# RG-LRU gates in TensorE's two row halves, with rope, w_mod and norm steps moved in a two-layer hybrid encoder

## The chip, the cores and the metric

One core of a Trainium2 chip runs the whole kernel. The metric is the time of one execution on the device, in microseconds (us); the program has one launch. The engines are TensorE (PE, with its weight loads shown apart as PEld), VectorE (DVE), ScalarE (ACT), GpSimd (POOL) and SyncE (SP, which here only issues DMAs).

## The reference

Two groups of 256 tokens go through two layers with shared weights, all in float32. One layer, cut to what the change touches:

```python
def rglru_branch(x_in, gate_in, conv_w, conv_b, w_a, b_a, w_i, b_i, lam):
    xc = dwconv_centred(x_in, conv_w, conv_b)
    xb = xc.reshape(B, S, RG_BLOCKS, RG_BW)            # 8 heads of 64
    def direction(d, reverse):
        r = sigmoid(einsum('bsnc,ncd->bsnd', xb, w_a[d]).reshape(B, S, RG_WIDTH) + b_a[d])
        i = sigmoid(einsum('bsnc,ncd->bsnd', xb, w_i[d]).reshape(B, S, RG_WIDTH) + b_i[d])
        ...
def encoder_layer(x, c, cos, sin, p):
    mod = (silu(c) @ p['w_mod'] + p['b_mod'])[:, None, :]
    sh1, sc1, gt1, sh2, sc2, gt2 = split(mod, 6, axis=-1)
    h = rmsnorm(x, p['ln1_g']) * (1 + sc1) + sh1
    ...                                  # h @ w_in, attention with rope, RG-LRU, gated DeltaNet
    x = x + gt1 * (mixed @ p['w_out'])
    h2 = rmsnorm(x, p['ln2_g']) * (1 + sc2) + sh2
    up = dwconv_centred(h2 @ p['ffn_w_up'], p['ffn_conv_w'], p['ffn_conv_b'])
    x = x + gt2 * ((silu(u_gate) * u_lin) @ p['ffn_w_down'])
```

## The kernel before

Both groups are laid side by side, so an activation tile is 128 channels by 512 tokens. A weight matrix is cut into **units** of 128 x 128, and the units of a layer stand in the order in which they are used; eight make a **chunk** of 512 KB. A chunk is loaded by SP into a `raw` buffer (four of them), cast by ACT to a high part `wh`, and DVE forms the low part `wl`. A unit then takes three matmuls (`mm3`): high weight on high and on low activations, low weight on high. `gemm` runs eight units into one PSUM bank; the pool `mm` has three banks, and ACT or DVE must have read a bank before a later job takes it. A chunk's load is issued two chunks ahead, and ACT's cast is called for six units ahead of use.

The order on TensorE and on SP is written by the program itself. `JOBS` lists the gemms of a layer: `in6` (first projections), attention (`uq`, `uk`, `uv`), the gated DeltaNet (`gq`, `gk`, `gv`, `z`), RG-LRU (`x` input, `g` gate, `b.i.d` recurrence gates of block i and direction d), `gate`, `br` (branches), `out`, `up`, `down`. Between units a `Driver` polls small generator tasks: attention steps, the DeltaNet chain (`solve`, `combine`: tiles `gdn_*`), and the modulation. Each task yields an estimated delay from `SLACK` or an event, and runs when the driver's own clock `now` has passed it. ACT, DVE and POOL are ordered by the framework's scheduler.

**Modulation.** `mod_gen` computes silu(c) @ w_mod. A w_mod chunk is four matmuls with 32 weight columns each, one in each quarter of TensorE's columns (tile `mod`, eight records in the trace). When a group of four blocks' columns is done, ACT copies the bank (`modev`), and four small matmuls select the rows (`mod<-cs,modev`). Layer 0 runs blocks 0 to 3 at the start; both layers run 4 to 9 (24 chunks) during the branches, one chunk every 8 us and loaded through the same `raw` buffers as the weights; 10 and 11 run in the norm ahead of `up` from `oraw` tiles. Blocks 0 to 3 of layer 1 run during `down` of layer 0 and in the norm behind it. Work in `drv.spare` is run wherever the driver has to wait.

**Gates of RG-LRU** (`rg_scan`): two heads of 64 are put on the diagonal of a 128 x 128 unit, one unit for w_a and one for w_i, three matmuls each, into banks `zr` and `zi`; ACT reads each with one tanh of 128 x 512.

**Rope** (`query`, `place`): DVE rotates the queries into tile `rope`; SP writes them to DRAM (`drope`) and back into `Qt`, at times that the driver's clock sets.

**Norms**: a sum of squares by TensorE, DVE's reciprocal square root (`tsx`), a matmul that spreads it over the partitions (`norm<-cs,tsx`), and `modulated`: DVE multiplies, ACT scales and shifts (`hn`), POOL makes the high part `hh`, DVE the low part `hl`.

Of the kernel before, what the change touches and what calls it, by code (L numbers as in the profile page):

```python
# [18 lines left out]
P = 128  # L19
T = 512  # L20
S = 256
# [21 lines left out]
def jobs():  # L43
# [10 lines left out]
        "gate": 8, "br": 4, "x": 8, "g": 8, "b": 2, "z": 8, "out3": 24, "out": 8, "up3": 24, "up": 8,  # L54
# [5 lines left out]

SLACK = {
    "modev": 0.7, "att_s": 3.2, "att_t": 1.8, "att_e": 1.0, "low_rank": 11.8, "low_rank_out": 152.5, "mla": 0.2,
# [3 lines left out]
    "rg_all": 16.0, "ssq": 6.5, "kq": 8.0, "norm": 2.8, "normed": 17.0, "mod1": 8.0, "mod2": 8.0,  # L66
# [75 lines left out]
class Driver:  # L142
# [12 lines left out]
    def spawn(self, gen):  # L155
        self.tasks.append([self.now, gen])
        self.poll()
# [12 lines left out]
    def poll(self):  # L170
        for task in list(self.tasks):
            if task in self.tasks and self._ready(task[0]):
                self._step(task, self.tasks)

# [61 lines left out]
def _body(es, tc, nc, xT, cT, wall, wmod, pvec, fng, cst, rope, xinit, yT, dbg):  # L236
# [348 lines left out]
    def modulated(l, which, x, r, k, g, h, pool, bufs):  # L585
        modT, modA = mods[l]
        c = GS[g]
        scale, bias = modA[:, which, k, g:g + 1], modT[:, 24 * which + k, g:g + 1]
        t = pool.tile([P, S], F32, name="hn", tag="hn", bufs=bufs)
        mul(t, x[:, c], r)  # L590
        A.activation(t, t, AF.Identity, bias=bias, scale=scale)  # L591
# [3 lines left out]
        split(t, h[k][0][:, c], h[k][1][:, c], pool=True)  # L595
# [45 lines left out]
    def hs(h):  # L641
        return [h[k] for k in range(8)]
# [71 lines left out]
    for l in range(depth):  # L714
# [84 lines left out]
        def query(j):  # L799
            if j == 0:  # L800
                drv.until(ev_cq)
            ps = gemm(cq)
            if j < 4:
                A.activation(Qt[0:64, 2 * j, :], ps[0:64], AF.Copy, scale=96.0 ** -0.5)
                A.activation(Qt[0:64, 2 * j + 1, :], ps[64:128], AF.Copy, scale=96.0 ** -0.5)
                return
            cosq, sinq = rep2(rt_[:, 0, :]), rep2(rt_[:, 1, :])
            if j == 4:
                lr["rope"] = mp.tile([P, 4, T], F32, name="rope", tag="Vt")
            ab = lr["rope"][:, 2 * j - 8:2 * j - 6, :]  # L810
            mul(halves(ab[:, 0, :]), halves(ps), cosq)
            mul(halves(ab[:, 1, :]), halves(ps), sinq)
            if j == 5:
                x, y = lr["rope"][:, 0:2, :], ab
                sub(x[:, 0, :], x[:, 0, :], y[:, 1, :])
                add(x[:, 1, :], x[:, 1, :], y[:, 0, :])

                def place():
                    yield SLACK["rope"]
                    dr = dp.tile([P, 2, T], F32, name="drope", tag="drope")  # L820
                    nc.sync.dma_start(dr, x)
                    yield SLACK["rope_out"]
                    for e in range(2):
                        nc.sync.dma_start(Qt[64 + 16 * e:80 + 16 * e], dr.rearrange("(h p) e t -> e p h t", p=16)[e])
                    ev_q.set(SLACK["rope_in"])
                drv.spawn(place())
# [102 lines left out]
        def rg_scan(i, d):  # L929
# [3 lines left out]
            zr = gemm([(xh, xl)])  # L933
            zi = gemm([(xh, xl)])
# [7 lines left out]
            A.activation(s, zr, AF.Tanh, bias=pr["hb"][:, c:c + 1], scale=0.5)  # L942
            A.activation(u, zi, AF.Tanh, bias=pr["hb"][:, 8 + c:9 + c], scale=0.5)
# [130 lines left out]
        def ahead():  # L1074
            yield from modulation(l + 1, ((0, 1),), SLACK["mod2"], next_raw, 8)
            drv.spare.append([0.0, modulation(l + 1, ((2, 3),), 0.0, next_raw, 8)])
# [3 lines left out]
        for job in JOBS:  # L1080
# [15 lines left out]
            elif k in ("gq", "gk", "gv"):  # L1096
                if k == "gq" and ix[0] >= 2:
                    drv.until(gdn.ev_free[ix[0] - 2])
                drv.spawn(gdn.part(k[1], ix[0], gemm(hs(h))))
            elif k == "uq":  # L1100
# [20 lines left out]
            elif k == "close":  # L1121
# [11 lines left out]
                drv.spawn(modulation(l, ((4, 5, 6, 7), (8, 9)), SLACK["mod1"], branch_raw, 1))  # L1133
# [24 lines left out]
            elif k == "close2":  # L1158
# [6 lines left out]
                def oraw(l, i):  # L1165
                    raw = rp.tile([P, UC * P], F32, name="oraw", tag="oraw", bufs=8)
                    nc.sync.dma_start(raw, wmod[l, i])
                    return raw
                drv.spare.append([0.0, modulation(l, ((10, 11),), 0.0, oraw, 8)])
# [3 lines left out]
            elif k == "out":  # L1173
# [5 lines left out]
                elif (d, g) == (7, 1):  # L1179
                    wait(SLACK["norm"])  # L1180
                    for us in sq.scale(1):
                        wait(us)
                    for k in range(8):
# [435 lines left out]
def mod_groups(l):  # L1619
    return ([(0, 1), (2, 3)] if l else [(0,), (1,), (2,), (3,)]) + [(4, 5, 6, 7), (8, 9), (10, 11)]  # L1620
# [9 lines left out]
def pack(inp):  # L1630
# [11 lines left out]
    for l in range(depth):  # L1642
# [17 lines left out]
        blk = np.zeros((4, 2, 2, P, P), np.float32)  # L1660
        for e, nm in enumerate(("rg_w_a", "rg_w_i")):
            w = f[nm][l].reshape(2, 4, 2, 64, 64)
            for s in range(2):
                blk[:, :, e, 64 * s:64 * s + 64, 64 * s:64 * s + 64] = w[:, :, s].transpose(1, 0, 2, 3)
# [76 lines left out]
```

## Time and profile before

| | us |
|---|---|
| median of 3 runs (1968.69 to 1971.42) | 1968.8 |
| the profiled execution | 1969.03 |
| its span, first to last instruction | 1966.9 |
| TensorE busy / VectorE / ScalarE / GpSimd | 1928.6 / 1238.5 / 822.5 / 255.5 |

Busy times overlap. A matmul's record is longer than its share of the stream, because the next one starts before it ends: the distance from start to start is what one costs. The chain of waits follows the work that ended last backwards; the idle time before an instruction is put down to the engine that released it.

### The profile page before, as it was taken

To read this page: it belongs to the slowest core of one execution; us is meant where nothing else is said; L and a number is where in the kernel's file an instruction comes from. 1 tells how busy PE (TensorE), PEld (TensorE's weight loads), DVE (VectorE), ACT (ScalarE), POOL (GpSimd) and SP (SyncE) were. 2 spreads that over 40 slices of the span, in tenths; PEclk is the share of its full clock that TensorE was granted. 3 is DMA by queue.
4 is the path that set the end of the run, shared out by engine and by line. 5 is a ranking of instruction groups with operands and counts; after the bars stand their busy time and mean duration, and the time that the engine had idled before them with its cause. 6 is when DMAs were issued, how large, how long until landed. Compare 5 with 4: busy or idle time off the path is not lost.

```text
span 1966.9 us, 29250 instructions
## 1 busy us (share of the span) xinstructions
PE 1928.6 (98%) x11435; PEld 1547.0 (79%) x11435; DVE 1238.5 (63%) x2328; ACT 822.5 (42%) x1275; POOL 255.5 (13%) x512
## 2 busy tenths in 40 slices
PE   9999999999999999999999999999999999999998
PEld 5877777777888888887877777777778878888887
DVE  5665787784366766653357758878644676666434
ACT  4444376532334444432234534756223354444322
POOL 1100163143001000000011003613410010000000
PEclk9999999999999999999999999999999999999999
DMA  8231354354253333353533224444532523233332
GB/s 326 65 118 53 101 147 115 113 141 119 76 205 106 97 97 97 96 187 112 189 112 97 65 65 125 111 142 119 142 96 91 208 91 97 94 104 90 104 97 97
DMA packets 141994, 231.43 MB, mean 118 GB/s; under 512 B 79776, under 2 KB 84512, under 8 KB 141856
## 3 DMA queue, kind: packets, MB, share of 16 engines
q1 hardware_dynamic: 136240, 221.95, 36.6%
q10 hardware_dynamic: 5616, 7.61, 1.1%
q8 instruction: 90, 1.47, 0.3%
q14 instruction: 48, 0.39, 0.1%
HBM read 221.66 MB, written 7.86 MB: 117 GB/s over the span
## 4 chain that ended last, share of the span: by engine, by line
PE 89%; DVE 4%; DMA 2%; ACT 1%; issue 1%; POOL 1%; SPq 0%; DVEq 0%; POOLq 0%; ACTq 0%
PE mm_up L221 25%; PE mm_gate L221 13%; PE mm_down L221 12%; PE mm_br L221 7%; PE mm_in L221 4%; PE mm_out L221 3%; PE mod L221 2%; PE mm_z L221 2%; PE mm_gq L221 2%; PE mm_x L221 2%; PE mm_gv L221 2%; PE mm_g L221 2%; PE att_s L221 2%; PE gdn_rec L221 1%; PE gdn_l L221 1%
## 5 line engine op out<-in xcount | busy, mean ns | idle before, releaser
L301 DVE TENSOR_TENSOR wl<-raw,wh 128x1024 fp32r<-128x1024 f32 x304 | 375.5, 1236 | 305.3 <-ACT wh L394 294.5
L394 ACT CAST wh<-raw 128x1024 fp32r<-128x1024 f32 x304 | 318.3, 1049 | 445.7 <-PE mm_down L221 127.6
L221 PE MATMUL mm_up<-hh,wh 128*128 128x512 f32 x704 | 276.7, 393 | 3.5 <-POOL hh L311 3.5
L221 PE MATMUL mm_up<-hl,wh 128*128 128x512 f32 x704 | 276.3, 392 | 0.0
L221 PE MATMUL mm_up<-hh,wl 128*128 128x512 f32 x704 | 275.9, 392 | 0.0
L304 DVE SCALAR_TENSOR_TENSOR cv<-mm_up,pv,cv 128x510 f32<-128x510 f32 x176 | 131.2, 748 | 61.2 <-ACT cv L574 58.0
L221 PE MATMUL mm_gate<-hh,wh 128*128 128x512 f32 x384 | 160.6, 418 | 0.0
L221 PEld LDWEIGHTS mm_up<-hh,wh 128*128 128x128 f32 x704 | 133.5, 190 | 31.8 <-POOL hh L311 3.9
L221 PEld LDWEIGHTS mm_up<-hl,wh 128*128 128x128 f32 x704 | 133.5, 190 | 28.2 <-DVE hl L301 0.3
L221 PEld LDWEIGHTS mm_up<-hh,wl 128*128 128x128 f32 x704 | 133.6, 190 | 27.7
L221 PE MATMUL mm_gate<-hh,wl 128*128 128x512 f32 x384 | 150.2, 391 | 0.0
L221 PE MATMUL mm_gate<-hl,wh 128*128 128x512 f32 x384 | 150.1, 391 | 0.0
L221 PE MATMUL mm_down<-ah,wh 128*128 128x512 f32 (+1 forms) x396 | 146.0, 369 | 0.0
L221 PE MATMUL mm_down<-ah,wl 128*128 128x512 f32 (+1 forms) x396 | 144.9, 366 | 0.6 <-DVE wl L301 0.6
L221 PE MATMUL mm_down<-al,wh 128*128 128x512 f32 (+1 forms) x396 | 144.8, 366 | 0.0
L311 POOL TENSOR_SCALAR hh<-hn 128x256 fp32r<-128x256 f32 x64 | 34.0, 544 | 686.6 <-ACT hn L591 685.9
L574 ACT ACTIVATE cv<-mm_up,pv 128x512 f32<-128x512 f32 x88 | 68.5, 780 | 89.4 <-PE mm_up L221 89.4
L221 PEld LDWEIGHTS mm_down<-ah,wh 128*128 128x128 f32 x396 | 74.7, 189 | 15.0 <-issue 3.3
L221 PEld LDWEIGHTS mm_gate<-hh,wh 128*128 128x128 f32 x384 | 72.2, 188 | 18.0 <-issue 4.9
L221 PEld LDWEIGHTS mm_down<-ah,wl 128*128 128x128 f32 x396 | 74.7, 189 | 12.9 <-DVE wl L301 0.8
L221 PEld LDWEIGHTS mm_gate<-hh,wl 128*128 128x128 f32 x384 | 72.1, 188 | 16.0
L221 PEld LDWEIGHTS mm_down<-al,wh 128*128 128x128 f32 x396 | 74.7, 189 | 11.8
(394 smaller groups left out, 3802.4 us busy)
## 6 DMA issues: line engine op xcount, KB each, us to landing
raw<-in_wall_dram SPq DMA_DIRECT2D x304, 512.0 KB, 3.6
raw<-in_wmod_dram SPq DMA_DIRECT2D x48, 512.0 KB, 3.6
mraw<-in_wmod_dram SPq DMA_DIRECT2D x16, 512.0 KB, 9.8
oraw<-in_wmod_dram SPq DMA_DIRECT2D x16, 512.0 KB, 7.0
hraw<-in_wmod_dram SPq DMA_DIRECT2D x32, 256.0 KB, 5.5
x<-in_xT_dram SPq DMA_DIRECT2D x8, 256.0 KB, 5.3
W<-dx SPq DMA_DIRECT2D x32, 64.0 KB, 3.9
xr<-in_xT_dram ACTq DMA_DIRECT2D x8, 256.0 KB, 3.6
```

Of the source, the lines that this page charges most:

```text
L221: return self.pe.matmul(out, lhsT, rhs, **kw)
L301: (eng or V).tensor_tensor(out, a, b, ALU.subtract)
L304: V.scalar_tensor_tensor(out, a, s, b, op0, op1)
L311: G.tensor_scalar(hi, x, 1.0, 0.0, ALU.mult, ALU.add)
L394: A.copy(wh, raw)
L574: A.activation(dst, ps, AF.Identity, bias=bias, scale=w[lo])
```

## The change

- **Gates.** One unit holds four 64 x 64 blocks; in each row half stand one head's w_a and w_i, in swapped columns for the second head. Six matmuls of 64 rows run, alternating between the row halves, each half into its own bank. ACT reads the two banks with four tanh of 64 partitions. A `b` job is one unit instead of two, so a layer has one chunk less.
- **w_mod.** In the branches layer 0 runs blocks 4 to 7, layer 1 blocks 6 and 7; layer 1's blocks 4 and 5 go to `down` of layer 0 and the norm behind it. Blocks 8 and 9 go with 10 and 11 into the norm ahead of `up`, from 16 `oraw` buffers that are loaded one by one during `out`. In the branches a chunk is run behind another task's step, or when it is 3.5 us overdue.
- **Rope.** SP's two steps are put behind `gq.0` and `gk.0` by place, not by the clock.
- **Norms.** For the first two of eight tiles POOL is left out: DVE multiplies and scales, ACT writes `hh`, DVE forms `hl`.
- Some entries of `SLACK` change, among them `W` and `kq`.

```diff
@@ SIZE, SLACK
-... "b": 2 ...                     +... "b": 1 ...
-"W": 4.0 ... "kq": 8.0 ... "mod1": 8.0, "mod2": 8.0
+"W": 5.2 ... "kq": 9.2 ... "mod1": 6.0, "mod2": 5.0, "oraw": 2.4
@@ Driver.poll
-        for task in list(self.tasks):
-            if task in self.tasks and self._ready(task[0]):
+        ran = False
+        for task in sorted(self.tasks, key=lambda task: task[2] > 0):
+            if task in self.tasks and self._ready(task[0]) and (ran or task[0] + task[2] <= self.now
+                                                                if task[2] else True):
                 self._step(task, self.tasks)
+                ran = True
@@ modulated
+        hi, lo = h[k][0][:, c], h[k][1][:, c]
+        if k < 2:
+            stt(t, x[:, c], scale, r, ALU.mult, ALU.mult)
+            A.activation(hi, t, AF.Identity, bias=bias)
+            stt(lo, t, bias, f32(hi), ALU.add, ALU.subtract)
+            return
@@ query
-                    yield SLACK["rope"]
                     nc.sync.dma_start(dr, x)
-                    yield SLACK["rope_out"]
+                    yield
...
-                drv.spawn(place())
+                lr["place"] = place()      # next() after gq.0 and after gk.0
@@ rg_scan
-            zr = gemm([(xh, xl)])
-            zi = gemm([(xh, xl)])
+            w, zs = unit(), [bank(), bank()]
+            for k, (wi, xi) in enumerate(((0, xh), (0, xl), (1, xh))):
+                for e, z in enumerate(zs):
+                    sl = slice(64 * e, 64 * e + 64)
+                    PE.matmul(z, w[wi][sl], xi[sl], start=(k == 0), stop=(k == 2))
+            drv.now -= 0.6
+            drv.poll()
-            A.activation(s, zr, AF.Tanh, bias=pr["hb"][:, c:c + 1], scale=0.5)
-            A.activation(u, zi, AF.Tanh, bias=pr["hb"][:, 8 + c:9 + c], scale=0.5)
+            for t, o, b in ((s, 0, c), (u, 64, 8 + c)):
+                for e, z in enumerate(zs):
+                    sl, zl = slice(64 * e, 64 * e + 64), slice(o ^ (64 * e), (o ^ (64 * e)) + 64)
+                    A.activation(t[sl], z[zl], AF.Tanh, bias=pr["hb"][sl, b:b + 1], scale=0.5)
@@ ahead, close, close2
-            yield from modulation(l + 1, ((0, 1),), SLACK["mod2"], next_raw, 8)
-            drv.spare.append([0.0, modulation(l + 1, ((2, 3),), 0.0, next_raw, 8)])
+            yield from modulation(l + 1, ((0, 1), (2, 3)), SLACK["mod2"], next_raw, 8)
+            drv.spare.append([0.0, modulation(l + 1, ((4, 5),), 0.0, next_raw, 8)])
-                drv.spawn(modulation(l, ((4, 5, 6, 7), (8, 9)), SLACK["mod1"], branch_raw, 1))
+                drv.spawn(modulation(l, ((6, 7) if l else (4, 5, 6, 7),), SLACK["mod1"], branch_raw, 1), LAZY)
-                drv.spare.append([0.0, modulation(l, ((10, 11),), 0.0, oraw, 8)])
+                def last_blocks():
+                    for i in range(32, 48):
+                        loaded[l, i] = oraw(l, i)
+                        yield SLACK["oraw"]
+                    scale2.append(mod_gen(l, ((8, 9),), 0.0))
+                    drv.spare += [[0.0, scale2[0]], [0.0, mod_gen(l, ((10, 11),), 0.0)]]
```

The queue of SP in layer 0, from the loads behind `in6` to the branches; `raw<-in_wall_dram` are weight chunks. Before:

```order
L381 DMA raw<-in_wall_dram 128x1024 x10
L821 DMA drope<-rope 128x1024
L824 DMA Qt<-drope 16x8x512 x2
L381 DMA raw<-in_wall_dram 128x1024 x16
L1062 DMA raw<-in_wmod_dram 128x1024
```

and now:

```order
L388 DMA raw<-in_wall_dram 128x1024 x12
L833 DMA drope<-rope 128x1024
L388 DMA raw<-in_wall_dram 128x1024
L836 DMA Qt<-drope 16x8x512 x2
L388 DMA raw<-in_wall_dram 128x1024 x13
```

Two weight chunks now stand ahead of the rope's write, and one between it and the read back. ScalarE at the same place, from `uk.0` on (`wh` is a chunk's cast, `gc` and `kq` belong to `gq.0` and `gk.0`). Before:

```order
L1107 COPY Kt<-mm_uk 64x512 x2
L394 CAST wh<-raw 128x1024
L572 ACTIVATE gc<-mm_gq,pv 128x512
L1107 COPY Kt<-mm_uk 64x512
L1313 ACTIVATE kq<-gc 128x512
L572 ACTIVATE gc<-mm_gk,pv 128x512
L1313 ACTIVATE kq<-gc 128x512
L394 CAST wh<-raw 128x1024 x2
```

and now:

```order
L1130 COPY Kt<-mm_uk 64x512 x2
L401 CAST wh<-raw 128x1024
L579 ACTIVATE gc<-mm_gq,pv 128x512
L401 CAST wh<-raw 128x1024
L1130 COPY Kt<-mm_uk 64x512
L1346 ACTIVATE kq<-gc 128x512
L401 CAST wh<-raw 128x1024
L579 ACTIVATE gc<-mm_gk,pv 128x512
```

Two casts have moved ahead of the work of `gq.0` and `gk.0`. TensorE at job `b.2.0` of layer 0, with what each instruction waits for. Before:

```order
L221 MATMUL mm_b<-xch,wh 128x512
L221 MATMUL mm_b<-xcl,wh 128x512
L221 MATMUL mm_b<-xch,wl 128x512
L221 MATMUL gdn_rec<-r,Y 128x128 [waits DVE_49,PE_49]
L221 MATMUL gdn_rec<-r,Y 128x128 [waits DVE_49]
L221 MATMUL gdn_rec<-r,Y 128x128 x2
L221 MATMUL mm_b<-xch,wh 128x512
L221 MATMUL mm_b<-xcl,wh 128x512
L221 MATMUL mm_b<-xch,wl 128x512
L221 MATMUL mm_gate<-hh_307,wh 128x512 [waits Activation_49]
```

and now:

```order
L228 MATMUL mm_b<-xch,wh 128x512 x2
L228 MATMUL mm_b<-xcl,wh 128x512 x2
L228 MATMUL mm_b<-xch,wl 128x512 x2
L228 MATMUL mm_gate<-hh_305,wh 128x512 [waits PE_49,Activation_49]
L228 MATMUL mm_gate<-hl_306,wh 128x512
```

The chain step that stood between the two halves is gone from there, and the next gemm follows at once, in the bank that the first of the two row halves has just filled.

## Rows read from the trace of the kernel before

**Rows 1.** The page: busy time by engine, and the chain that ended last.
```profile
PE 1928.6 (98%) x11435; PEld 1547.0 (79%) x11435; DVE 1238.5 (63%) x2328; ACT 822.5 (42%) x1275; POOL 255.5 (13%) x512
...
PE 89%; DVE 4%; DMA 2%; ACT 1%; issue 1%; POOL 1%; SPq 0%; DVEq 0%; POOLq 0%; ACTq 0%
```

**Rows 2.** Who PE waited for: waiter <- releaser: us in total, times, longest.
```profile
PE mm_uk L221 <- ACT wh L394: 9.6, 2, 4.8
...
PE gdn_l L221 <- DMA W<-dx: 1.3, 1, 1.3
PE mm_out L221 <- DVE wl L301: 1.1, 2, 0.5
```

**Rows 3.** Timeline of PE at `uk.3`: start us, length, instruction [idle before <-releaser].
```profile
115.09 0.80 PE L221 MATMUL mm_uk<-ch,wh 128*128 128x512 f32 x1 [4.78 <-ACT wh L394]
...
118.22 0.63 PE L221 MATMUL mm_uv<-wh,ch 128*128 128x512 f32 x1
```

**Rows 4.** Timeline of ACT in the same stretch.
```profile
113.47 0.63 ACT L1313 ACTIVATE kq<-gc 128x512 f32<-128x512 f32 x1 [2.44 <-DVE gc L304]
114.00 1.03 ACT L394 CAST wh<-raw 128x1024 fp32r<-128x1024 f32 x1
```

**Rows 5.** What SP's queue waited for, 60 to 130 us.
```profile
SPq L821 <- DVE rope L301: 22.0, 1, 22.0
```

**Rows 6.** Two stretches: busy by engine (instructions), then granted clock, DMA share, GB/s.
```profile
115.10:119.10 4.00, 3.96 (x9) 2.67 (x10) 2.36 (x3) 1.46 (x2) 0.00 (x0) 0.50 0.43 128
...
620.95:627.70 6.75, 6.01 (x14) 4.68 (x15) 5.01 (x14) 3.76 (x7) 2.75 (x6) 0.50 0.00 0
```

**Rows 7.** Timeline of PE around job `b.0.0`.
```profile
250.75 0.39 PE L221 MATMUL mm_x<-hh,wl 128*128 128x512 f32 x1
...
252.11 0.39 PE L221 MATMUL mm_b<-xch,wl 128*128 128x512 f32 x1
252.60 0.50 PE L221 MATMUL mm_g<-hh,wh 128*128 128x512 f32 x1
```

**Rows 8.** Timeline of PE around one w_mod chunk inside a gemm of the branches.
```profile
246.53 0.40 PE L221 MATMUL mm_x<-hh,wl 128*128 128x512 f32 x1
246.86 0.64 PE L221 MATMUL mod<-raw,csil 128*32 128x256 f32 x8
247.43 0.50 PE L221 MATMUL mm_x<-hh,wh 128*128 128x512 f32 x1
247.77 0.39 PE L221 MATMUL mm_x<-hl,wh 128*128 128x512 f32 x1
```

**Rows 9.** Timeline of ACT and DVE: reading the banks of `x.1` and `b.0.0`.
```profile
251.18 0.78 ACT L574 ACTIVATE xc<-mm_x,pv 128x512 f32<-128x512 f32 x1 [1.83 <-PE mm_x L221]
251.86 0.69 ACT L942 ACTIVATE rs<-mm_b,p_hb 128x512 f32<-128x512 f32 x1
252.54 0.69 ACT L943 ACTIVATE ru<-mm_b,p_hb 128x512 f32<-128x512 f32 x1
...
254.04 0.74 DVE L304 SCALAR_TENSOR_TENSOR xc<-mm_x,pv,xc 128x508 f32<-128x508 f32 x1
```

**Rows 10.** Timeline of ACT: an operation on 64 partitions.
```profile
77.65 0.60 ACT L805 ACTIVATE Qt<-mm_uq 64x512 f32<-64x512 f32 x1
```

**Rows 11.** Timeline of PE and POOL in the norm ahead of `up`, layer 0.
```profile
612.39 2.80 PE L221 MATMUL mod<-oraw,csil 128*32 128x256 f32 x48
...
616.55 1.07 PE L221 MATMUL mod<-oraw,csil 128*32 128x256 f32 x16
...
618.33 1.06 PE L221 MATMUL mod<-cs,modev 128*128 128x4 f32 x8 [0.70 <-ACT modev L516]
619.24 0.69 PE L221 MATMUL norm<-cs,tsx 128*128 128x128 f32 x4
621.69 0.80 PE L221 MATMUL mm_up<-hh,wh 128*128 128x512 f32 x1 [1.76 <-POOL hh L311]
...
621.24 2.03 POOL L311 TENSOR_SCALAR hh<-hn 128x256 fp32r<-128x256 f32 x4 [3.76 <-ACT hn L591]
```

More of the change, by code (lines that the diff above doesn't have):

```diff
@@ L53 @@
 SIZE = {"in6": 48, "gq": 8, "gk": 8, "gv": 8, "uq": 3, "uk": 2, "pad": 2, "uv": 8,
-        "gate": 8, "br": 4, "x": 8, "g": 8, "b": 2, "z": 8, "out3": 24, "out": 8, "up3": 24, "up": 8,
+        "gate": 8, "br": 4, "x": 8, "g": 8, "b": 1, "z": 8, "out3": 24, "out": 8, "up3": 24, "up": 8,
         "down": NFF, "close": 0, "mid": 0, "close2": 0}
@@ L58 @@
 NCH = -(-NU // UC)
+LAZY = 3.5
 SLACK = {
@@ L63 @@
     "rg_x": 0.8, "ab": 5.7, "softplus": 13.7, "gates": 4.7, "v": 5.8, "ws": 3.0, "z": 0.2, "gw":
[2 rows of a table removed]
-    "rg_all": 16.0, "ssq": 6.5, "kq": 8.0, "norm": 2.8, "normed": 17.0, "mod1": 8.0, "mod2": 8.0,
[2 rows of a table added]
+    "rg_all": 16.0, "ssq": 6.5, "kq": 9.2, "norm": 2.8, "normed": 17.0, "mod1": 6.0, "mod2": 5.0, "oraw": 2.4,
     "kd": 0.1, "start": 0.6, "diag2": 4.6, "cq": 2.1, "lr_diag": 5.3, "diag": 30.4}
@@ L153, in event, with spawn @@
         return Event(self)
-    def spawn(self, gen):
-        self.tasks.append([self.now, gen])
+    def spawn(self, gen, lazy=0.0):
+        self.tasks.append([self.now, gen, lazy])
         self.poll()
@@ L589, in modulated @@
         t = pool.tile([P, S], F32, name="hn", tag="hn", bufs=bufs)
-        mul(t, x[:, c], r)
-        A.activation(t, t, AF.Identity, bias=bias, scale=scale)
         if k not in h:
@@ L594, in modulated @@
                     hp.tile([P, T], F32R, name=f"hl{k}", tag=f"hl{k}"))
-        split(t, h[k][0][:, c], h[k][1][:, c], pool=True)
+        hi, lo = h[k][0][:, c], h[k][1][:, c]
[4 more added lines that the diff above has]
+            return
+        mul(t, x[:, c], r)
+        A.activation(t, t, AF.Identity, bias=bias, scale=scale)
+        split(t, hi, lo, pool=True)
     class Norm:
@@ L825, in place @@
                     ev_q.set(SLACK["rope_in"])
-                drv.spawn(place())
+                    yield
+                lr["place"] = place()
         def values():
@@ L1099, in _body @@
                 drv.spawn(gdn.part(k[1], ix[0], gemm(hs(h))))
+                if ix[0] == 0 and k != "gv":
+                    next(lr["place"])
             elif k == "uq":
@@ L1165, in oraw @@
                 def oraw(l, i):
-                    raw = rp.tile([P, UC * P], F32, name="oraw", tag="oraw", bufs=8)
+                    raw = rp.tile([P, UC * P], F32, name="oraw", tag="oraw", bufs=16)
                     nc.sync.dma_start(raw, wmod[l, i])
                     return raw
-                drv.spare.append([0.0, modulation(l, ((10, 11),), 0.0, oraw, 8)])
+                def last_blocks():
[4 more added lines that the diff above has]
+                    drv.spare += [[0.0, scale2[0]], [0.0, mod_gen(l, ((10, 11),), 0.0)]]
+                scale2 = []
+                drv.spawn(last_blocks())
             elif k == "out3":
@@ L1182, in _body @@
                         wait(us)
+                    while any(t[1] is scale2[0] for t in drv.spare):
+                        drv._step(drv.spare[0], drv.spare)
                     for k in range(8):
@@ L1619, in mod_groups @@
 def mod_groups(l):
-    return ([(0, 1), (2, 3)] if l else [(0,), (1,), (2,), (3,)]) + [(4, 5, 6, 7), (8, 9), (10, 11)]
+    return ([(0, 1), (2, 3), (4, 5), (6, 7)] if l else [(0,), (1,), (2,), (3,), (4, 5, 6, 7)]) + [(8, 9), (10, 11)]
 def _units(w):
@@ L1659, in pack @@
         up = _units(f["ffn_w_up"][l]).reshape(2, NFF, 8, P, P).transpose(1, 0, 2, 3, 4).reshape(2 * NFF, 8, P, P)
[L1660 removed]
+        blk = np.zeros((4, 2, 1, P, P), np.float32)
         for e, nm in enumerate(("rg_w_a", "rg_w_i")):
@@ L1663, in pack @@
             for s in range(2):
-                blk[:, :, e, 64 * s:64 * s + 64, 64 * s:64 * s + 64] = w[:, :, s].transpose(1, 0, 2, 3)
+                o = 64 * (e ^ s)
+                blk[:, :, 0, 64 * s:64 * s + 64, o:o + 64] = w[:, :, s].transpose(1, 0, 2, 3)
         def side(w):
```

4 rows, old and new, of the table SLACK are left out of this document.

## The prediction

> **What bounds the kernel now.** I read the page first: TensorE is busy for 98% of the span and carries 89% of the chain that ended last [rows 1]. So time can only go in two ways: less work on TensorE, or fewer of the places where it stands still or runs at its lower clock. A matmul of 512 columns costs its step from start to start: from the last matmul of `x.1` to the last of `b.0.0` lie six steps in 1.36 us, 0.227 each [rows 7]. The list of waits then names the largest stall, `uk.3` waiting for ACT's cast of its chunk, 4.8 us in each layer [rows 2]. The timeline around it shows why: PE stands from 110.31 to 115.09, and ACT starts the cast at 114.00, at once behind `kq` of `gk.0`, which waited for DVE [rows 3, 4]. That chunk's load was late as well: SP stood 22 us before the rope's write, until DVE had made the rope, with weight loads queued behind [rows 5]. After such a stall the granted clock is 0.50, the level of 1.2 GHz, and nine matmuls take 4.0 us [rows 6]. The norm ahead of `up` is the second such place [rows 6, 11].
>
> **Rope's place: -13.7.** The load of the chunk of `uk.3` now stands ahead of the rope's write on SP, and ACT's cast ahead of both `kq`s. From the start of the stall to the end of `uk.3` pass 7.9 us [rows 3] for six matmuls that need 1.36: 6.6 a layer, and 0.4 more in the first layer where `uv` starts at the half clock (two matmuls at 0.43 [rows 3, 6]). What is late next: `att_s` needs `Qt`, whose read back waits for the rope as before, and with the stall gone attention comes some 7 us earlier. Between `gk.0` and attention still lie `uk.3` and `uv`, 30 matmuls or 6.8 us, and the read back is issued ahead of that, so I count nothing. Two layers: -13.7, and 0 if something else is late there.
>
> **Gates: -5.6.** 16 jobs of six full matmuls, 1.36 us each, become three rounds of two half-height ones. No row shows two row halves at work, so I bound it. A w_mod chunk, four matmuls side by side in column quarters, is the nearest: the step into it is 0.33, it takes 0.57 for two rounds, and the first matmul behind it 0.34 [rows 8]. Against 0.227 that is 0.10 to enter, 0.57 - 0.45 = 0.12 to leave and 0.11 behind. A gate job with halves that overlap as those quarters do: 0.10 + 3 x 0.227 + 0.12 + 0.11 = 1.01, so -0.35 each. If the halves ran one after the other it would be 1.69, +0.33 each, +5.3 in all; without any cost of entering it would be -0.68 each, -10.9. I take the chunk's row, as the nearest. The Trainium skill's page TensorEngine Tiling (Array Packing), section Theoretical Speedup, promises up to 2x for a dimension of 64 or less; by it the term would be the -10.9, but the chunk's row shows 0.33 of switching on top of its two rounds.
>
> **What the gates add: +11.8.** ACT now reads the two banks with four operations, first half of both gates last: the first bank is free after the third, where before the first bank was free after one. An operation on 128 partitions takes 0.69 and starts 0.68 behind the one before [rows 9], one on 64 partitions 0.60 [rows 10], so halving the partitions halves nothing. The three banks of the pool decide who waits. Behind `b.0.0` and `b.2.0` the next gemm is given the bank of the first row half. ACT starts 0.43 after the job's last matmul starts (252.11 to 252.54 [rows 7, 9]); three operations later, 2.5 us, the bank is free. Behind `b.2.0` the gemm would start after 0.34: a wait of 2.2. Behind `b.0.0` a w_mod chunk fills 0.67 of it, and 0.26 of waiting is there already (252.11 to 252.60 [rows 7]): +1.3. Behind `b.1.1` the next gemm gets the bank of `x.2`, which DVE's convolution holds: for `x.1` the last read ended 4.0 us after its last matmul started (250.75 to 254.78 [rows 7, 9]), and only 32 small matmuls and the job itself stand between, about 1.5 us: +2.4. That is 5.9 a layer. Queued behind these waits are all of PE's work, the DeltaNet chain's steps among it. If ACT is early or the small steps longer, it is less; 0 is the other end.
>
> The same page, section Performance Considerations, says of the PSUM bottleneck that tiling speeds up TensorE but not the evacuation of PSUM. It speaks against this change; it gives no time, and by it this term is not the 0.
>
> **w_mod: -5.5.** A chunk inside a gemm costs 0.67 between the matmuls around it and 0.11 on the next one, 0.78 [rows 8]. 24 chunks leave the branches (8 in layer 0, 16 in layer 1): -18.7. Eight more run inside `down` of layer 0: +6.2, and one more group's selection, 0.9 (618.33 to 619.24 [rows 11]). Eight more run in each norm ahead of `up`. There six chunks took 2.80, 0.47 each [rows 11]. They stand between the selection and the spread: the spread, at 619.24, moves to 622.9, since eight chunks take 3.7. From the spread to `up` were 2.45 us; POOL's 0.41 goes [rows 11], DVE's `hl` adds about as much for the second matmul: 2.4. So `up` starts 3.6 later, +7.2 for two layers. Loads one by one in place of eight at once should end the 1.1 us of waits in `out` [rows 2]. Sum: -18.7 + 6.2 + 0.9 + 7.2 - 1.1 = -5.5. That chunks now run behind chain steps, in place of cutting a gemm alone, is worth at most the 0.1 of an entry each; I count nothing.
>
> **Small ones: -2.3.** A longer `W` slack ends the wait for that DMA, -1.3 [rows 2]. Without POOL the first tile at the start and between the layers comes about 0.5 earlier each, -1.0 (0.41 of POOL and its hand-over [rows 11]).
>
> **Clock: -2.8.** Ahead of `up` 14 matmuls took the 6.0 us from 621.69 to 627.70, at the half clock, where 3.2 would do [rows 6, 11]: 2.8 a layer. PE stood 0.70 and 1.76 before that [rows 11]; now more of the stretch is filled with chunks, and only about 2 us of selection, spread and waits are left at its end. I take one of the two spells as gone; both or none are as easily so.
>
> Sum: -13.7 - 5.6 + 11.8 - 5.5 - 2.3 - 2.8 = -18.1. The profiled execution took 1969.0 (span 1966.9 and 2.1 around it), 0.2 over the median of 1968.8; 1969.0 - 18.1 = **1951**.
>
> **Rivals.**
> 1. *The banks are free in time* (the waits behind the three jobs stay under 1 us): 1951 - 11.8 = 1939, and 1936 if both half-clock spells go. For it: ACT is busy for 42% only. Against: three operations of 0.6 to 0.69 cannot end in the 0.34 that the gemm needs.
> 2. *The row halves run one after the other*: the gates cost +5.3 in place of -5.6, 1962. For it: each half needs its own weight load, and weight loads are busy 79% already [rows 1]. Against: the four quarters of a chunk plainly overlap.
> 3. *The rope's stall moves rather than goes*: attention or the next cast waits instead, 1951 + 13.7 = 1965. For it: ACT still has `kq` between casts, and DVE's chain behind `gk.0` is unchanged. Against: the two chunks of `uk.3` and `uv` are cast ahead of it.
> 4. *Slower: the clock falls at the gate jobs.* A long stand of PE is followed by the half clock [rows 3, 6], which costs about 2.8 a time. If half of the 16 jobs brought a wait of 2.2 and such a fall, that is 8 x 5.0 = 40 in place of 11.8: 1979. It decides from about six such falls on (18 us). Against: these waits are half as long as the stall of 4.78 [rows 3], and matmuls stand close around them.
> 5. *It does not do what it says*: the last chunks of w_mod come too late for the norm, since DVE's first step of `modulated` now needs the scale that they give. The selection stands eight chunks ahead of the spread, so I put this with the small chances.
>
> **How the numbers follow.** The forecast (1945 to 1957) has 0.49; rival 1 0.24; rival 2 0.13; rival 3 0.05; rival 4 0.04; faster than all, 1925 to 1936, with the dearer ends gone and the gates cheaper 0.03; rival 5 at about the old time 0.02. Eight in ten reach from 1934 to 1962: below is only the rarest case, above are 3 to 5. A measurement of this kernel tells 0.2% from no change, 3.9 us: faster means under 1964.9. Faster: 0.49 + 0.24 + 0.13 + 0.03 and a part of rival 3, 0.92; the same 0.04; slower 0.04.
>
> **What would show it.** Right: PE's wait for ACT's `wh` at `uk.3` is gone and the clock stays at 1.00 there; the gate matmuls come in pairs with a step of about 0.23 a pair; PE waits about 2 us for ACT's `ru` behind `b.0.0` and `b.2.0` and for DVE's `xc` behind `b.1.1`, in both layers; `up` starts about 13 us after `out` ends rather than 9. Wrong: steps of 0.23 for a single gate matmul (rival 2); no wait behind the gate jobs (rival 1); a new wait at `att_s` or `uv` (rival 3); more than six stretches at 0.50 between 230 and 560 us (rival 4).

## The result and the profile after

The changed kernel takes 1992.8 us (median of 4 runs, 1991.7 to 1995.0) against 1969.6 of the kernel before: a ratio of 1.0113, interval 1.0101 to 1.0125. It is 23 us slower, and the prediction was 18 us faster. The profiled execution has a span of 1989.9 us against 1966.9. The page's busy times and chain, as [rows 1] before:

```profile
PE 1925.3 (97%) x11443; PEld 1542.6 (78%) x11443; DVE 1242.5 (62%) x2326; ACT 844.7 (42%) x1306; POOL 247.6 (12%) x496
...
PE 85%; DVE 8%; ACT 3%; POOL 1%; DMA 1%; issue 1%; SPq 0%; DVEq 0%; POOLq 0%; ACTq 0%
```

TensorE is busy for 3 us less, in a span that is 23 us longer; on the chain DVE has 8% where it had 4%. So the time went into places where TensorE stands, and into a lower clock (below). The list of its waits (waiter, releaser, us in total, times, longest), as [rows 2]:

```profile
PE mm_up L228 <- DVE hn L302: 15.4, 2, 7.7
PE mm_gv L228 <- DVE wl L308: 5.6, 2, 3.5
PE mm_x L228 <- DVE wl L308: 5.6, 2, 2.8
PE mm_gate L228 <- ACT ru L964: 4.9, 2, 2.7
PE mm_gate L228 <- DVE xc L311: 4.1, 2, 2.0
PE mm_g L228 <- ACT ru L964: 3.2, 2, 1.6
...
PE mm_b L228 <- DVE xcl L308: 1.7, 2, 1.0
...
PE gdn_l L228 <- DMA W<-dx: 1.4, 1, 1.4
```

The wait of `uk.3` for `wh` is gone. Two new kinds of wait have come: in `up`, and in the branches between `x` and `out`.

**uk.3.** TensorE's timeline there, as [rows 3]: the last matmul of `gk.0`, and `uk.3` right behind it, at the full clock.

```profile
110.28 0.39 PE L228 MATMUL mm_gk<-hh,wl 128*128 128x512 f32 x1
110.51 0.39 PE L228 MATMUL mm_uk<-ch,wh 128*128 128x512 f32 x1
110.74 0.39 PE L228 MATMUL mm_uk<-cl,wh 128*128 128x512 f32 x1
```

**The branches.** The stretch from the first `x` matmul to the first `out` matmul, layer 0 and layer 1; columns: stretch, its length, busy us of PE, PEld, DVE, ACT, POOL (instructions), granted clock, DMA share, GB/s. The kernel before:

```profile
237.30:565.83 328.53, 324.85 (x2574) 256.37 (x2572) 223.12 (x452) 153.56 (x245) 99.12 (x202) 1.00 0.42 117
1206.80:1535.33 328.53, 325.02 (x2573) 256.40 (x2572) 221.17 (x427) 153.59 (x245) 96.87 (x202) 1.00 0.42 117
```

and the changed one:

```profile
230.95:569.55 338.60, 323.10 (x2510) 254.48 (x2509) 225.37 (x447) 164.26 (x259) 99.18 (x202) 0.97 0.36 99
1219.73:1549.31 329.58, 314.10 (x2446) 250.27 (x2444) 221.19 (x418) 164.16 (x259) 100.76 (x202) 0.99 0.33 89
```

Length less busy time is where TensorE stands: 3.7 and 3.5 us before, 15.5 and 15.5 now. ACT has 10.7 us more to do in each layer. The granted clock falls to 0.50 in four stretches of layer 0 (from 248.1, 278.9, 289.1 and 405.2, 17.1 us together) and in two of layer 1 (6.8 us); before it never fell there. Two of these stretches, of the same columns:

```profile
289.12:292.50 3.38, 3.38 (x54) 2.38 (x55) 3.09 (x5) 2.92 (x8) 2.99 (x5) 0.50 0.35 73
405.20:411.90 6.70, 5.87 (x14) 4.62 (x15) 5.77 (x8) 3.73 (x5) 5.92 (x11) 0.50 0.40 116
```

Only those from 248.1 and 289.1 begin in a wait for a gate job's bank (1.6 us behind `b.0.0`, 2.0 behind `b.1.1`). The other two of layer 0 and both of layer 1 begin in a wait for `wl`, or up to 1.3 us behind it (2.8 and 3.5, then 2.8 and 2.2).

One gate job, undisturbed (`b.3.1`, timeline of TensorE), and ACT's reads of another:

```profile
385.89 0.40 PE L228 MATMUL mm_gate<-hh,wl 128*128 128x512 f32 x1
386.22 0.50 PE L228 MATMUL mm_b<-xch,wh 64*128 64x512 f32 x2
386.56 0.40 PE L228 MATMUL mm_b<-xcl,wh 64*128 64x512 f32 x2
386.79 0.39 PE L228 MATMUL mm_b<-xch,wl 64*128 64x512 f32 x2
387.11 0.50 PE L228 MATMUL mm_gq<-hh,wh 128*128 128x512 f32 x1
387.45 0.39 PE L228 MATMUL mm_gq<-hl,wh 128*128 128x512 f32 x1
```

```profile
246.28 1.39 ACT L964 ACTIVATE rs<-mm_b,p_hb 64x512 f32<-64x512 f32 x2 [1.43 <-PE mm_b L228]
247.70 1.39 ACT L964 ACTIVATE ru<-mm_b,p_hb 64x512 f32<-64x512 f32 x2
```

The matmuls come in pairs. From 385.89 to 387.45 pass 1.56 us; two full steps of 0.227 would stand there without the job, so the job costs 1.10, against 1.36 before. ACT's operations on 64 partitions take 0.69 each, as those on 128 did [rows 9].

The wait behind `b.2.0`, as it stands in TensorE's timeline:

```profile
314.91 0.40 PE L228 MATMUL mm_b<-xch,wl 64*128 64x512 f32 x2
317.49 0.50 PE L228 MATMUL mm_gate<-hh,wh 128*128 128x512 f32 x1 [2.19 <-ACT ru L964]
```

**up.** `up` starts 57.5 us after `out` starts, where it was 55.9 and 55.6. Then TensorE does the first tile for two of the three gemms of `up3`, and stands:

```profile
628.65 0.39 PE L228 MATMUL mm_up<-hh,wl 128*128 128x512 f32 x1
636.74 0.80 PE L228 MATMUL mm_up<-hh,wh 128*128 128x512 f32 x1 [7.70 <-DVE hn L302]
```

DVE at the end of that wait:

```profile
636.27 0.41 DVE L302 TENSOR_TENSOR hn<-x,norm 128x256 f32<-128x256 f32 x1
```

TensorE goes on when this `hn` ends, at 636.68. No matmul reads `hn`. But DVE reads `norm`, group 0's spread over the partitions, which lies in a PSUM bank, and this is the last tile's multiplication for group 0. In the built program the third gemm of `up3` has that very bank, in both layers: `gemms` takes its three banks from the pool `aux` of five, and the selection and the sums of blocks 8 and 9, which the change put into this norm, have taken two more of them since the bank of the spread was given out. Before, the third bank was that of the selection, which had long been read.

From start to start, `up` to `down` is 249.7 us in both layers, 242.3 and 242.4 before. The half clock at the start of `up` is gone: the first six matmuls run at the full clock. It comes inside the new wait instead, for 6.8 us from 633.9 in layer 0 and from 1613.5 in layer 1.

### The profile page after: what moved, and what is told of

The parts are those of the page before. It is cut to its first block, busy times and chain, and to the rows that moved or that the text cites. A ratio compares the mean times of both kernels' runs of the same rounds, so it can differ in the third digit from the quotient of the medians.

```text
span 1989.9 us, 29298 instructions
## 1 busy us (share of the span) xinstructions
PE 1925.3 (97%) x11443; PEld 1542.6 (78%) x11443; DVE 1242.5 (62%) x2326; ACT 844.7 (42%) x1306; POOL 247.6 (12%) x496
## 4 chain that ended last, share of the span: by engine, by line
PE 85%; DVE 8%; ACT 3%; POOL 1%; DMA 1%; issue 1%; SPq 0%; DVEq 0%; POOLq 0%; ACTq 0%
PE mm_up L228 24%; PE mm_down L228 12%; PE mm_gate L228 12%; PE mm_br L228 6%; PE mm_out L228 4%; PE mm_in L228 3%; PE mod L228 3%; PE mm_z L228 2%; PE mm_g L228 2%; PE mm_gv L228 2%; PE att_s L228 2%; PE mm_gq L228 1%; PE mm_uq L228 1%; PE gdn_rec L228 1%; DVE wl L308 1%; PE mm_x L228 1%
## 5 line engine op out<-in xcount | busy, mean ns | idle before, releaser
L318 POOL TENSOR_SCALAR hh<-hn 128x256 fp32r<-128x256 f32 x48 | 22.5, 477 | 706.5 <-ACT hn L607 705.5
L228 PEld LDWEIGHTS mm_down<-al,wh 128*128 128x128 f32 x396 | 74.7, 189 | 11.6
```

The costliest lines, as they stand in the source:

```text
L228: return self.pe.matmul(out, lhsT, rhs, **kw)
L318: G.tensor_scalar(hi, x, 1.0, 0.0, ALU.mult, ALU.add)
```

## The experiments

Times are medians, ratios to the kernel before measured beside it. "x to out" is the stretch of the rows above.

**The rope's place alone**, on the kernel before.

```diff
                 def place():
-                    yield SLACK["rope"]
...
-                    yield SLACK["rope_out"]
+                    yield
...
-                drv.spawn(place())
+                lr["place"] = place()      # next() behind gq.0 and gk.0
```

> The kernel before, with the rope's place of the change alone. Theory: the stall at uk.3 goes and nothing takes its place, as in the changed kernel's trace (gate to uv 43.5 us in place of 50.2, in each layer): 13.4 us less, about 1956. Rival (moves): the stall goes elsewhere, 1965 to 1970.

1957.5, ratio 0.9936 (0.9919 to 0.9952). `gate` to `uv` takes 43.49 us in both layers where it took 50.21, and nothing behind it grew by more than 1.0. The theory holds.

**The gates undone in the changed kernel, and the gates alone on the kernel before.** The first takes `rg_scan`, `SIZE["b"]` and the packing of the blocks back, the second brings them in.

```diff
-            w, zs = unit(), [bank(), bank()]
...
+            zr = gemm([(xh, xl)])
+            zi = gemm([(xh, xl)])
```

> The changed kernel with the block-diagonal gates of before; all else is kept. Theory (gates): all waits that are new in the branches come from the gates, by their banks and by the shorter jobs, and the clock falls behind these waits. From the first x to out it then takes the time of before less its w_mod chunks: 322.3 us in layer 0 (338.6 with the row halves) and 316.0 in layer 1 (329.6); about 1963. Rival (w_mod): the new order of the w_mod chunks, behind other steps, makes the waits; then these stretches stay at 335 to 342 and 327 to 333, about 1995.

> The kernel before, with the gates of the change alone. Taking the gates out of the changed kernel gave 21 us. Theory (gates by themselves): the same waits come here, and the time is 1985 to 1992. Rival (together with w_mod): the 24 w_mod chunks that before still runs between the units give ScalarE and VectorE the time that they need; then the waits are smaller and the time is 1968 to 1978.

Undone: 1971.9, 20.9 less than the changed kernel. Alone: 1990.7, ratio 1.0104 (1.0089 to 1.0119). With the gates undone:

```profile
232.74:559.45 326.71, 320.68 (x2510) 255.94 (x2509) 225.18 (x448) 154.04 (x244) 100.05 (x202) 0.99 0.37 104
1209.24:1528.63 319.39, 313.65 (x2445) 253.39 (x2444) 221.79 (x419) 153.42 (x244) 102.62 (x202) 1.00 0.34 94
```

That is 11.9 and 10.2 us less than with the row halves, and 12.1 and 10.0 is what the gates alone add to the kernel before. So the gates lose as much by themselves. The waits are not all the same, though: alone, TensorE stands 2.2, 3.8 and 1.0 us at the three banks in each layer and 0.3 for `wl` in `mm_x`, where the changed kernel has 1.6, 2.0 and 2.2 or 2.7, and 2.8. The 322.3 and 316.0 of the theory were not reached: in layer 0 there is a wait of 2.8 us for a w_mod load, with 3.4 us at the half clock behind it. Layer 1 keeps the full clock; waits for `wl` and `xcl` make TensorE stand 2.2 us longer there than before, and the 16 chunks took 11.4 us of its busy time with them (325.0 to 313.7), 0.71 each and not 0.78.

**Banks from the other pool.** The changed kernel, gates in banks of `aux`.

```diff
-            w, zs = unit(), [bank(), bank()]
+            w, zs = unit(), [aux_tile(name="mm_b"), aux_tile(name="mm_b")]
```

> The changed kernel, with the two banks of a gate job taken from the five of the pool aux in place of the three of mm; the four reads are kept. Theory (banks): what the row halves cost is that the next gemm waits for a bank; with other banks the three waits behind gate jobs, 5.8 and 6.3 us, go with the half clock behind them, x to out takes about 328 us in layer 0 (338.6) and 322 in layer 1 (329.6), about 1976. Rival (load): the four reads also delay all that ScalarE and VectorE do next, and the waits come back behind later jobs, as waits for xc, wl or xcl; both stretches stay within 4 us of what they were, 1987 or more.

1978.6, ratio 1.0044 (1.0029 to 1.0059).

```profile
232.74:562.24 329.50, 319.30 (x2510) 251.34 (x2509) 224.95 (x447) 164.03 (x259) 101.83 (x202) 0.99 0.36 102
1212.43:1533.84 321.41, 311.07 (x2446) 248.19 (x2445) 220.34 (x418) 163.94 (x259) 101.24 (x202) 1.00 0.33 91
```

All three waits behind gate jobs are gone, and 9.1 and 8.2 of the 11.9 and 10.2 us come back, with the four reads still there: TensorE stands 5.3 and 5.1 us less, and is busy for 3.8 and 3.0 us less, with 6.8 us at the half clock in layer 0 and none in layer 1. The theory holds for most of it. The waits for `wl` are still there in both layers:

```profile
PE mm_x L228 <- DVE wl L308: 2.8, 1, 2.8
PE mm_gv L228 <- DVE wl L308: 2.2, 1, 2.2
```

Only one of these four is followed by the half clock here, that in `mm_x` of layer 0.

**Fewer reads.** The changed kernel, two tanh of 128 partitions a job.

```diff
-            for t, o, b in ((s, 0, c), (u, 64, 8 + c)):
-                for e, z in enumerate(zs):
...
+            A.activation(s, zs[0], AF.Tanh, bias=pr["hb"][:, c:c + 1], scale=0.5)
+            A.activation(u, zs[1], AF.Tanh, bias=pr["hb"][:, 8 + c:9 + c], scale=0.5)
```

> The changed kernel, but ScalarE reads the two banks of a gate job with two tanh of 128 partitions, as before, in place of four of 64. That gives wrong gates: half of the values end in the other gate's place. The matmuls, the banks and the order on TensorE are kept. Theory (reads): the two more operations of 0.69 us per job are what makes the waits behind the gate jobs, delays all that ScalarE and VectorE do next (the low halves wl among it) and so drops the clock; without them x to out takes 322 to 325 us in layer 0 (338.6 with four reads, 326.7 with the gates of before) and 317 in layer 1, about 1968. Rival (halves): the cause is that the shorter jobs leave less cover, whoever reads; the waits stay, and the time is 1985 or more.

1974.4, x to out 324.9 and 322.5. Most of the loss goes here too, but fewer reads also free the banks sooner (the wait behind `b.2.0` is 0.8 us in place of 2.2 in layer 0), so this alone doesn't separate the reads from the banks.

**Old places for the chunks.** A gate job takes a second, unused unit.

```diff
+            unit()
             drv.now -= 0.6
```

> The changed kernel, with a second, unused unit of zeros in every gate job, so that a b job takes two units of a chunk as before and every later weight chunk begins at the unit at which it began before. The row halves and their banks are kept. Theory (chunks): the waits for DVE's wl (2.8 and 3.5 us in layer 0; 2.8, 1.5 and 2.2 in layer 1) come from the places at which the chunks now begin; they go, with the half clock behind four of them, and the three waits behind gate jobs stay: 12.8 for the waits and some 8 for the clock less, about 1972. Rival (DVE): the wl waits come of DVE's own load once w_mod is out of the way; they stay, wherever the chunks begin, and the time stays at 1988 to 1996.

1995.4, x to out 340.6 and 327.7. The waits for `wl` in `mm_x` went, but waits for banks came in their place (2.3 us behind `b.1.0` for ACT's `gt`, 2.7 in place of 2.0 behind `b.1.1`), and the sum stayed. The time is the rival's, but not for its reason. While the banks bind, the old places bring nothing.

**Banks and places, then the reads too.** On the version that took 1954.1 (further down: gates of before, one bank of `up3` from `mm`, no short rule in the norm), the gates of the change with both edits; and the same with two reads.

```diff
-            zr = gemm([(xh, xl)])
-            zi = gemm([(xh, xl)])
+            w, zs = unit(), [aux_tile(name="mm_b"), aux_tile(name="mm_b")]
...
+            unit()
```

> The version with the bank for up3 and without the short rule in the norm, which took 1954.1 with the gates of before, now with the row halves, their banks from the pool aux, and an unused second unit in every gate job, so that chunks begin where they did before. Theory (banks and places): what the row halves cost beside their banks is the new places of the chunks, for which the waits for wl stood behind x.2 (2.8 us) with the banks from aux; with both cured only the shorter job is left, 8 x 0.26 = 2.1 us a layer for it: x to out at most 326 us in layer 0 and 318 in layer 1, about 1950. Rival (reads): ScalarE's two more reads a job keep VectorE's steps late, and waits for wl and xc stay: 321 us or more in layer 1, 1955 or more.

> The same, and with two reads of 128 partitions in place of four of 64 (half of the gate values then end in the other gate's place). Nothing but the matmuls of the row halves differs now from the version at 1954.1. Theory (work): the shorter job alone is worth 2.1 us a layer, x to out 326 us or less in layer 0 and 317.7 in layer 1. Rival (order): what the driver's clock makes of the shorter jobs decides, and the stretches differ from that by more than 2 us either way.

1955.7, ratio 0.9926 (0.9909 to 0.9944), and 1955.4, 0.9930 (0.9905 to 0.9954). With the four reads, x to out, and below it the version with the gates of before:

```profile
230.55:557.42 326.87, 317.91 (x2510) 250.66 (x2509) 227.09 (x448) 164.48 (x260) 101.34 (x202) 0.99 0.37 104
1199.90:1520.35 320.45, 312.99 (x2446) 249.27 (x2445) 222.01 (x419) 164.36 (x260) 100.19 (x202) 0.99 0.34 93
```

```profile
230.69:558.78 328.09, 321.93 (x2509) 256.56 (x2508) 225.39 (x448) 154.02 (x244) 99.95 (x202) 0.99 0.37 104
1201.13:1520.96 319.83, 313.68 (x2445) 253.38 (x2444) 222.04 (x419) 153.30 (x244) 102.47 (x202) 1.00 0.33 94
```

The whole loss is gone, so banks and places together made it. The two more reads by themselves cost nothing that shows: with two, the stretches take 325.9 and 322.1, the second again over what was expected. Nor do the row halves gain: TensorE stands 9.0 and 7.5 us in place of 6.2 and 6.1, which takes back the shorter jobs. Layer 1 missed the 318 expected; the waits that came are for other steps, `vs` of the DeltaNet chain (1.3) and `wl` (2.2) among them.

**The order of the reads.** Both reads of the first bank first, in the gates of the change; the rest is the version at 1954.1.

```diff
-            for t, o, b in ((s, 0, c), (u, 64, 8 + c)):
-                for e, z in enumerate(zs):
+            for e, z in enumerate(zs):
+                for t, o, b in ((s, 0, c), (u, 64, 8 + c)):
```

> The gates of the change with the four reads in another order: both reads of the first bank, then both of the second. Beside that it has the bank for up3 and the norm without the short rule, so it stands against the version with the gates of before (1954). Theory (bank of the first half): the first bank is free one read of 0.69 earlier, so the waits behind b.0.0 and b.2.0 fall from 1.6 and 2.2 to about 0.9 and 1.5 in each layer; x to out takes 335 to 338 and 326 to 329, and the time is 1970 to 1974. Rival (chain): the exponential of the gate chain now waits for all four reads, and what the bank gives the chain takes back; x to out stays at 338.6 and 329.6, about 1975.

1969.1; x to out 332.7 and 329.3. The waits behind `b.0.0` fell from 1.6 to 0.9, those behind `b.2.0` from 2.2 and 2.7 to 1.5 and 2.0: by 0.7 each, one read, so the wait is for the bank's last read. Against the changed kernel, layer 0 fell by 5.9 us, and two of its four half-clock stretches went too; layer 1 hardly moved, with three such stretches in place of two. The theory was right on the waits; the clock made the rest of it go either way.

**A bank for up3.** The changed kernel; one of the three banks from `mm`.

```diff
-        pss = [bank() if i < n - 3 else aux_tile(...) for i in range(n)]
+        pss = [bank() if i < n - 2 else aux_tile(...) for i in range(n)]    # up3 alone
```

> The changed kernel, with one of the three PSUM banks of up3 taken from the pool mm in place of the pool aux. Theory (banks): in the changed kernel the third gemm of up3 gets the bank that holds group 0's spread, and DVE's multiplications hn read that until the eighth tile, so PE stands 7.7 us in each layer. With another bank the two stalls go: up takes about 242.4 us in place of 249.7 in each layer, 14.6 in all, about 1978. Rival (tiles): the second tile of the norm is simply late, since DVE and ACT now do POOL's share; then PE stands in front of the second tile still, and the time stays above 1988.

1981.8, 11 less. The stall of 7.7 went, but a smaller one came:

```profile
PE mm_up L228 <- DVE wl L308: 5.1, 2, 2.6
```

`up` takes 244.3 and 244.4. The theory was right on the cause and 2 us a layer short on what is late next.

**The norm's short rule out**, with that bank (and the gates undone), and without it.

```diff
-        if k < 2:
-            stt(t, x[:, c], scale, r, ALU.mult, ALU.mult)
...
-            return
```

> The changed kernel with the gates of before, one bank of up3 from mm, and without the rule for the first two tiles of the norms (POOL makes all high parts again). With the bank alone, up kept a wait of 2.5 us for DVE's wl in each layer and took 244.4 us; before it was 242.4. Theory (rule): DVE's extra steps on the first two tiles push wl back; without the rule the wait goes, up takes 242.4, and the time is about 1957 (1971.9, less 10.9 for the bank and 4 for the rule). Rival (place): wl comes late because up now starts later against DVE's queue; the wait stays, about 1961.

> The changed kernel with the gates of before and without the short rule in the norm; all three banks of up3 come from aux again, and the third is again group 0's spread. Theory (bank): the stall of 7.7 us in up is the bank's, whatever the rule; it stays, up takes 248 to 250 us in each layer, and the time is about 1970. Rival (both): the rule had moved the reads of the spread back, and without it they end early; the stall is under 4 us, and the time is 1962 or less.

With the bank: 1954.1, ratio 0.9913 (0.9899 to 0.9928), the lowest median of all. `up` takes 239.7 us in both layers, with no stall of note and no half clock:

```profile
PE mm_up L228 <- POOL hh L318: 0.9, 2, 0.5
```

Without it: 1971.3, and the stall is there, whatever the rule:

```profile
PE mm_up L228 <- DVE hn L302: 13.9, 2, 7.0
```

So the bank alone is worth 17 us once the rule is out. The rule brought the start of `up` 0.5 us forward and then cost 4.6 a layer, by the wait for `wl` (2.5) and the half clock.

**The w_mod chunks' pace.** Four versions with the gates undone and the bank: polled as before at 6 us (with the short rule still in); late polling at 8 us; the chain's writes 4 us later; polled as before at 8 us (all three without the rule).

```diff
-LAZY = 3.5        "mod1": 6.0        "X": 17.0
+LAZY = 0.0 | "mod1": 8.0 | "X": 21.0 | LAZY = 0.0, "mod1": 8.0
```

> The changed kernel with the gates of before and one bank of up3 from mm, and with the w_mod chunks of the branches polled as before: not behind another task's step, but when they are due. With the late polling there were waits in the branches of 2.8 us for a w_mod load in layer 0, with half clock behind it, and of 1.3 us for xcl in both layers. Theory (late polling): these go, 7 us, about 1954. Rival (no matter): they come of the smaller number of chunks, and the time is that of the two other edits, about 1961.

> The version with the gates of before, a bank of up3 from mm and the norm without the short rule (1954.1), with the w_mod chunks of the branches one every 8 us as before in place of 6. In layer 0 TensorE waited 3.0 us for a w_mod load that stood on SP behind the DeltaNet chain's write dx, and 6.8 us at half clock followed. Theory (queue): at the old pace that load is not behind dx, and 6.4 us go, about 1948. Rival (same place): another load stands there, 1952 to 1956.

> The same version (1954.1), with the pace of 6 us but with the DeltaNet chain's writes dx and what follows them 4 us later by the driver's clock (the entry X 21 in place of 17). Theory (queue): the w_mod load goes to SP ahead of the waiting dx, the wait of 3.0 us and the half clock behind it go, about 1948. Rival (chain): the chain's W then comes later and TensorE waits for it, 1952 or more.

> The version at 1954.1 (gates of before, a bank of up3 from mm, no short rule) with the w_mod chunks of the branches polled and paced as before, one every 8 us when due, but 8 and 16 fewer of them. Theory (order): TensorE's order up to the last remaining chunk is then that of before, whose waits were 3.7 us a layer, and what is left is the chunks taken out: x to out 322.3 us in layer 0 and 316 in layer 1 (328.1 and 319.8 at 1954.1), about 1945. Rival (chance): fewer chunks shift TensorE against the other engines' steps in any order, and other waits come; x to out takes over 325 and over 319, 1951 or more.

1970.6, 1957.4, 1963.1 and 1962.2: none gained, the first against the 1961 that its rival gives (its twin with late polling was not run), the others against 1954.1. The wait for a w_mod load, 3.0 us in the version at 1954.1, became 5.8 with the old polling at 6 us; in the others it went or fell to 0.5 or less, and other waits came. With the old polling and pace the profiled execution (the slowest of ten, 1970.2) took 334.5 us in layer 0's stretch, and TensorE waited there:

```profile
PE gdn_tr L232 <- DVE kq L311: 3.1, 2, 2.3
PE gdn_l L228 <- DMA W<-dx: 3.0, 1, 3.0
```

All four theories fell, the first by more than its rival said. What the runs have in common is that with fewer chunks TensorE comes to the other engines' steps earlier, and that which step is late then changes with the order; that the chunks were cover is how I read it, and no run shows it by itself.

## Why the prediction was wrong

Two steps failed. The prediction foresaw no wait in `up` beyond its first tile, where the third gemm's bank makes TensorE stand 7.7 us in each layer. And it let the bank waits in the branches add up and put nothing on what stands behind them: 11.6 us of other new waits came, mostly for `wl`, and some 8.5 us of half clock. The terms against the trace of after, in us:

| term | predicted | measured |
|---|---|---|
| rope's place | -13.7 | -13.4 |
| gate jobs | -5.6 | -4.2 (16 x 0.26) |
| three bank waits a layer | +11.8 | +12.2 |
| other new waits, x to out | -1.3 | +11.6 |
| half clock, x to out | 0 | +8.5 (estimate) |
| w_mod chunks out of the branches | -18.7 | -17.1 (estimate, 24 x 0.71) |
| w_mod in `down` | +7.1 | +7.2 |
| later start of `up` | +6.1 | +3.5 |
| `up` | -2.8 | +14.7 |
| norms at the start and between layers | -1.0 | -1.1 |
| `in6` behind these norms | 0 | +1.2 |

Standing time x to out rose by 23.8 (31.0 less 7.2), 12.2 of it the three waits and 10.0 waits for `wl` (12.8 where 2.8 were). For the work, a chunk is taken at the 0.71 that layer 1 shows with the gates undone, at the full clock. TensorE's busy time of before, 324.9 and 325.0, less 8 and 16 chunks and 8 jobs of 0.26, would be 317.1 and 311.6; it is 323.1 and 314.1, and I put these 8.5 down to the half clock. At 0.78 a chunk it would be 10.3.

- **Rope: right**, as the prediction put it, mechanism and size.
- **Gate jobs: right in kind**, 0.09 too cheap each: the first pair's step is 0.34, not 0.23, and the third with its cost of leaving 0.32, not 0.35. Rival 2 fell: the halves overlap. The Trainium skill's page TensorEngine Tiling (Array Packing), section Theoretical Speedup, has up to 2x; the trace gives 1.36 against 1.10, and no run here the 2x.
- **Bank waits: right**, by place and size (1.6, 2.0, 2.2 and 1.6, 2.0, 2.7). What failed is the step behind: that they add up and no more. The half clock came in six stretches, at some 1.4 us each where I had priced 2.8, and I had it in rival 4 with 0.04. But this is not that rival: its sign was more than six stretches in layer 0, where four came, and only two of the six begin at a gate job's bank. The Trainium skill's page TensorEngine Tiling (Array Packing), section Restrictions and Gotchas, says that row tiling raises the pressure on PSUM; the trace agrees: with banks from another pool 17 of the 22 us went.
- **Waits for `wl`:** not in the sum at all. A job of one unit moves where every later chunk begins; I had costed the chunk saved and not the places. The wait in `mm_x` (2.8) is gone in all three runs with the old places, though in the one with two reads 3.2 and 3.3 us for `wl` come in `mm_b`. With the gates alone on the kernel before it is 0.3, so it takes more of the change than the gates. The waits in `mm_gv` stay with the old places and four reads (2.4 and 2.2), and their cause is open. With the banks cured, the old places bring 329.5 and 321.4 to 326.9 and 320.5; that is one profile each, and two versions that differ in the norm and in `up3` alone have 326.7 and 328.1 in layer 0.
- **up: the step that failed most, by 17.5 us.** I followed the norm's engines and looked for the first tile's time; the sums and the selection of blocks 8 and 9 each take a bank of `aux`, and I did not follow that pool on to `up3`, as I had followed the three banks of `mm`. The half-clock stretch that I expected to lose in one layer went from its place in both, and came back in both inside the new wait.
- **w_mod: right as work** (chunks, `down`, start of `up`), too good as time: the version at 1954.1 has w_mod's and the rope's change, but neither the row halves nor the shared bank nor the short rule, and is 3 us below the rope alone (1957.5), with intervals that overlap. Out of the branches 17 us of chunks made the two stretches 9.1 us shorter.
- **Small ones: wrong in sum.** The first tiles came 0.6 and 0.5 us earlier, as forecast, but `in6` behind them took 1.0 and 0.3 longer; without the rule, in the version at 1971.3, it takes 44.9 and 34.4 us, as before. The rule also cost time in `up`, and the wait for `W` stayed (1.4 for 1.3).

Rivals 1, 3 and 5 did not occur. What stays open: which of TensorE's waits is followed by the half clock. That behind `b.2.0` in layer 0 (2.19) was not, that behind `b.0.0` (1.62, with another of 1.05 ahead of it) was. That behind `b.1.1` was in layer 0 (2.03) and not in layer 1 (2.04).

## What to carry to other kernels

Where a change adds tiles to a rotating pool, follow the pool beyond the change, up to the first tile that lands on one still being read; here two more small tiles put a gemm behind eight norm steps, and one number in the choice of banks was worth 17 us. Work on the bounding engine that is halved while its results take as long to read can cost more than it saves if the banks for them are those of the next gemm; here it saved nothing that shows with other banks either (1955.7 against 1954.1). And work taken out of a tightly ordered stretch need not be saved in full: ask which steps of the other engines it stood in front of.

## What the hardware showed beside that

- Two matmuls of 64 rows, in the two row halves, start 1 to 6 ns apart, one pair of the 48 15 ns; undisturbed, three pairs follow in steps of 0.34, 0.23 and 0.32 us, and the next full matmul costs 0.34 once.
- A tanh of 64 partitions x 512 takes as long as one of 128 (0.69).
- The clock's price behind a wait of 2.8 us, here in `mm_x` of layer 0: some 0.6 us after TensorE goes on, the steps grow from 0.23 to 0.43.

```profile
278.31 0.50 PE L228 MATMUL mm_x<-hh,wl 128*128 128x512 f32 x1 [2.80 <-DVE wl L308]
278.65 0.44 PE L228 MATMUL mm_x<-hh,wh 128*128 128x512 f32 x1
278.88 0.63 PE L228 MATMUL mm_x<-hl,wh 128*128 128x512 f32 x1
279.31 0.63 PE L228 MATMUL mm_x<-hh,wl 128*128 128x512 f32 x1
```
